# The output projection of a two-layer hybrid trunk, computed as seven quadrant products instead of one full product

## The chip, the cores and the metric

One core of one Trainium2 chip. The metric is the time of one execution on the device in microseconds (us); the median of several runs is compared. A profile is one such execution, recorded by the hardware profiler; its span goes from the first instruction to the last event.

## The reference

Two layers; each adds a mixer to the residual stream x of 512 tokens by 1024 features, all in float32:

```python
for l in range(2):
    h = rmsnorm(x, norm_g[l])
    p = h @ w_in[l]                       # 1024 -> 3488 columns, split into 15 parts
    o_a = causal attention (low-rank q and kv, rotary key)      # 256 columns
    o_b = c_b * short_conv(c_c * c_h)                           # 256
    o_c = spatial_gate(sg_u, sg_v)                              # 256
    o_d = block-sparse attention                                # 256
    y = concat(o_a * silu(g_a), o_b * silu(g_b), o_c * silu(g_c), o_d * silu(g_d))
    x = x + y @ w_out[l]                  # 512x1024 times 1024x1024
```

The change concerns the last line. Products have to keep nearly float32 precision.

## The kernel before, in words

**Numbers.** TensorE multiplies tiles of type fp32r, which hold fewer bits than float32. So each operand is split in two, `hi` (rounded by a copy into fp32r) and `lo` (the value less `hi`); `split2` (L245) does it with one copy on ScalarE (ACT) and one subtraction on VectorE (DVE). `mm3` (L250) then issues three matmuls for a product: hi by hi, hi by lo, lo by hi, all into one PSUM bank of 128 partitions by 512 columns.

**Layout.** Features lie on partitions: `hTh`, `hTl` hold the normed input h transposed, as 8 tiles of 128 features by 512 tokens. y is made the same way: `y_tiles` (L781) gives hi and lo of feature tile kt (0 and 1 from group A, 2 and 3 from B, 4 and 5 from C, 6 and 7 from D); `put_y` (L785) splits it and sets the event `L.y[kt]`. y4 to y7 come late; y5 is the last, made from `gc1`, the last product before the projection.

**Weights.** A `Unit` (L265) is a block of weights of up to 128x1024. `load_units` (L316) loads all units in one fixed order through two `raw` buffers (queue of SP), `split_units` (L331) splits each into one of six pairs `whi`, `wlo`, in halves of 512 columns: ACT makes `hi` (now and then DVE), DVE `lo`. A pair comes free when the last matmul that uses it is done. `w_out` is eight units per layer, `wo{half}{kq}`: half of the output columns, quarter of the features.

**The projection before** (L1229 to L1263): for each half of the output columns and each of four token tiles of 128, eight feature tiles times three matmuls of 512 columns, with y as the stationary and the weights as the moving operand: 192 matmuls per layer, into tiles named `o`. In the first half, token tiles 0 to 2 do six feature tiles first and the last two (y5, y7) afterwards. The very last token tile is cut into two passes of 256 columns. `out_chain` (L1145) then adds the bank to the residual tile `xr` on DVE; in layer 0 it also takes the sum of squares for the next norm (`square_half`, on ACT), stores x to DRAM and starts `pre_norm` (L544), which scales on DVE, transposes on TensorE and splits into `hTh`, `hTl`; in layer 1 it stores the output.

**Order.** A planner inside the kernel's Python code (`Order`, `Chain`, L58 to L193) writes out the order of the instructions on each engine. It has a clock per engine and a cost per instruction (TensorE n/2.4 + 2 ns, DVE 68 + 1.047 n, GpSimd 160 + 2.1 n, for n columns). Each chain of work is a generator that issues its next instruction when the clocks say that its input is nearly there. On the chip each engine works through its own list in that order and waits at semaphores. All instructions of DVE, ACT and GpSimd (POOL) are issued in one helper line, L158, those of TensorE (PE) in L184; so groups are told apart by their tiles.

**Buffers.** PSUM has three banks `acc`, two `tr` and three `s`, each handed out as slots. `t2` are nine 128x512 scratch tiles in SBUF; `tk` are two larger ones for Q and K of group A.

Of the kernel before, what the change touches and what calls it, by code (L numbers as in the profile page):

```python
# [38 lines left out]
YORDER, YCUT = (2, 3, 0, 1, 4, 6, 5, 7), 6  # L39
WORDER = (1, 0, 2, 3)  # L40
# [156 lines left out]
def hybrid_trunk(ctx: ExitStack, tc: tile.TileContext, x, positions, norm_g, w_c, w_f, w_t, w_o, mla_q_norm_g,  # L197
# [52 lines left out]
    def mm3(ch, n, dst, sh, sl, mh, ml, first, last):  # L250
        c = cost(n)
        yield from ch.pe(c, PE.matmul, dst, sh, mh, start=first, stop=False)
        yield from ch.pe(c, PE.matmul, dst, sh, ml, start=False, stop=False)
        yield from ch.pe(c, PE.matmul, dst, sl, mh, start=False, stop=last)
# [10 lines left out]
    class Unit:  # L265
        def __init__(self, src, a, b, name):
            self.src, self.a, self.b, self.name = src, a, b, name
            self.loaded, self.ready, self.wanted = Event(), Event(), False
            self.slots = eS if name[:-2] in EARLY else wS
# [31 lines left out]
    for l in range(DEPTH):  # L301
# [10 lines left out]
        for half in range(2):  # L312
            for kq in WORDER:
                add_unit(w_o[l, half, kq], 2, 512, f"wo{half}{kq}_{l}")

    def load_units():  # L316
        for u in order:
            ch = Chain(o)
            u.raw_slots = rawS
# [11 lines left out]
    def split_units():  # L331
        for u in order:
# [4 lines left out]
            for i in range(2):  # L337
# [11 lines left out]
                yield from c2.dve(V.tensor_tensor, lo, raw, hi.bitcast(F32), op=ALU.subtract)  # L349
            ch.t = c2.t  # L350
            u.raw_slots.put(ch)
            o.set(u.ready, ch.t)

# [27 lines left out]
    hTh = big.tile([P, KT, S], F32R, name="hTh")  # L381
    hTl = big.tile([P, KT, S], F32R, name="hTl")
# [128 lines left out]
    for l in range(DEPTH):  # L511
# [15 lines left out]
        L.mix_ev, L.mla_ev, L.QK_ev = Event(), Event(), Event()  # L527
        L.x = [None] * NT
# [15 lines left out]
    def pre_norm(L, t, xx, t0, release):  # L544
# [14 lines left out]
        if t == NT - 1:  # L559
            for _ in range(2):  # L560
                (t2S if L.l else sS).put(ch)

        def half(c):
            c2 = Chain(o, tps[c])
            tp = yield from trS.get(c2, f"hT{t}_{c}_{L.l}")
            for k in range(4):
# [3 lines left out]
            yield from split2(c2, hTh[:, c * 4:c * 4 + 4, t * P:(t + 1) * P],  # L570
                              hTl[:, c * 4:c * 4 + 4, t * P:(t + 1) * P], tp.rearrange("p (k n) -> p k n", k=4))
            trS.put(c2)
            o.set(L.hT[t][c], c2.t)
        for c in range(2):
            o.spawn(half(c))

# [79 lines left out]
    def q_chain(L, t, q_ps, t0):  # L656
        ch = Chain(o, t0)
        l = L.l
        if t == 0:
            L.Q = yield from tkS.get(ch, f"Q{l}", 96)  # L660
            L.K = yield from tkS.get(ch, f"K{l}", 96)
            o.set(L.QK_ev, ch.t)
# [122 lines left out]
    def put_y(ch, L, kt, yv):  # L785
        if kt == 6:
            L.yD = []
            for i in range(2):
                L.yD.append((yield from ydS.get(ch, f"yD{i}_{L.l}", [P, 2, S], F32R)))
        yield from split2(ch, *y_tiles(L, kt), yv)  # L790
        o.set(L.y[kt], ch.t)

# [352 lines left out]
    def out_chain(L, half, t, a, t0, c0=0, c1=512):  # L1145
        ch = Chain(o, t0)
# [4 lines left out]
        if l < DEPTH - 1:  # L1151
            yield from square_half(ch, layers[l + 1], t, half, a, L.x[t])
        accS.put(ch)
        if l == DEPTH - 1:
            nc.sync.dma_start(out[0, t * P:(t + 1) * P, cols], L.x[t][:, cols])
        elif half == 1:
            nc.sync.dma_start(x1d[t * P:(t + 1) * P, :], L.x[t])
            tend = ch.t + 4000.0

            def release(c):  # L1160
                c2 = Chain(o, max(c.t, tend))
                v4S.put(c2)
            o.spawn(pre_norm(layers[l + 1], t, L.x[t], ch.t, release))


    def main():
        m = Chain(o)

        def tok(L, n, width, t, dst, us):

            for k in range(KT):
                if n == "c" and k % 4 == 0:
                    yield from m.wait(L.hT[t][k // 4])
                if t == 0 and k % 2 == 0:
                    us.append((yield from unit(m, f"{n}{k // 2}_{L.l}")))
                wh, wlo = us[k // 2]
                yield from mm3(m, width, dst, hTh[:, k, t * P:(t + 1) * P], hTl[:, k, t * P:(t + 1) * P],
                               wh[:, k % 2, :], wlo[:, k % 2, :], k == 0, k == KT - 1)
                if t == NT - 1 and k % 2 == 1:
# [8 lines left out]
        for L in layers:  # L1188
# [8 lines left out]
            for t in range(NT):  # L1197
# [10 lines left out]
            for n in SEQ:  # L1208
# [10 lines left out]
                else:  # L1219
                    a = yield from accS.get(m, f"{n}_{l}")  # L1220
                    wh, wlo = yield from unit(m, f"{n}_{l}")
                    for k in range(KT):
                        yield from mm3(m, S, a, wh[:, k, :], wlo[:, k, :], hTh[:, k, :], hTl[:, k, :],
# [5 lines left out]
            for half in range(2):  # L1229
                us = {}  # L1230

                def part(t, a, i0, i1, c0=0, c1=512):
                    for i in range(i0, i1):
                        k = YORDER[i]
                        yield from m.wait(L.y[k])
                        if k // 2 not in us:
                            us[k // 2] = yield from unit(m, f"wo{half}{k // 2}_{l}")
                        wh, wlo = us[k // 2]
                        yh, yl = y_tiles(L, k)
                        yield from mm3(m, c1 - c0, a[:, c0:c1], yh[:, t * P:(t + 1) * P], yl[:, t * P:(t + 1) * P],  # L1240
                                       wh[:, k % 2, c0:c1], wlo[:, k % 2, c0:c1], i == 0, i == KT - 1)
                        if t == NT - 1 and c1 == 512 and all(x // 2 != k // 2 for x in YORDER[i + 1:]):
                            done_unit(f"wo{half}{k // 2}_{l}")
                        yield o.now

                acc = {}
                for group, cut in (((0, 1, 2), YCUT), ((3,), 0)) if half == 0 else (((t,), 0) for t in range(NT)):
                    for i0, i1 in ((0, cut), (cut, KT)):
                        for t in group:
                            if i0 == i1:  # L1250
                                continue
                            if i0 == 0:
# [130 lines left out]
```

## Time and profile before

| what | value |
|---|---|
| median of 3 runs | 508.73 us (508.62 to 508.78) |
| the profiled execution's own time | 508.65 us |
| span of its profile | 506.8 us |
| granted TensorE clock over the span | 0.996 |
| the first layer's projection in the trace | from 214.4 to 260.6 us |
| the second layer's projection in the trace | from 459.5 to 503.3 us |

A row of the page's groups reads: line, engine, operation, output and inputs by their names in the program, shapes, count, then busy time and the mean of one in ns, then the engine's idle time just before them and what ended it. PEld is TensorE's loading of the stationary operand, which runs beside the matmuls. In the rows of the timeline the first number is the start in the span, the second the time from the first to the last of the instructions merged into the row. Matmuls overlap, so their own durations are latencies and their pace is seen from their starts.

### The profile page before, as it was taken

Reading aid. Unit: us, or ns where it says so; the run is one execution under the profiler, and the core shown is the slowest. Engines: PE = TensorE matmul, PEld = TensorE weight load, DVE = VectorE, ACT = ScalarE, POOL = GpSimd, SP = SyncE. Lnnn points to the kernel's source line nnn. Section 1 sums busy time; section 2 is a strip of 40 time slices with the busy share of each in tenths; the row PEclk is TensorE's granted clock in tenths of the full one; section 3 lists DMA queues with packets and bytes.
Section 4 is the critical chain, followed back from the end, with each engine's and each line's share of the span. In section 5 each row is a group of like instructions: output and inputs, shape, how many; then the busy total and the mean of one; then the engine's idle time right before and its main releaser. Section 6 shows DMA issues by size and latency. Waiting matters only on the chain.

```text
span 506.8 us, 7665 instructions
## 1 busy us (share of the span) xinstructions
PE 498.1 (98%) x2508; PEld 423.3 (84%) x2508; DVE 349.3 (69%) x917; ACT 296.5 (58%) x891; POOL 139.2 (27%) x321
## 2 busy tenths in 40 slices
PE   6999999999999999999999999999999999999997
PEld 4898888888888888888889988888888888888886
DVE  4877975468799887635576988777868887635311
ACT  5698764567687775424247894677766777432100
POOL 6867875452000000000121488513330000000000
PEclk9999999999999999999999999999999999999999
DMA  8533415112114123464443242140142121624111
GB/s 273 165 123 114 125 43 166 41 43 66 60 43 166 52 74 109 142 175 117 143 155 126 83 125 71 55 124 2 42 167 82 43 83 49 201 84 164 66 54 50
DMA packets 20618, 51.57 MB, mean 102 GB/s; under 512 B 5985, under 2 KB 7265, under 8 KB 20578
## 3 DMA queue, kind: packets, MB, share of 16 engines
q1 hardware_dynamic: 20546, 51.08, 31.1%
q8 instruction: 20, 0.33, 0.3%
q0 software_dynamic: 32, 0.00, 0.1%
q14 instruction: 20, 0.16, 0.1%
HBM read 46.87 MB, written 4.19 MB: 101 GB/s over the span
## 4 chain that ended last, share of the span: by engine, by line
PE 90%; POOL 4%; DVE 2%; DMA 2%; ACT 1%; issue 1%; POOLq 0%; DVEq 0%
PE o L184 17%; PE kv L184 10%; PE cq L184 6%; PE sq L184 5%; PE cc L184 4%; PE gb L184 4%; PE cb L184 4%; PE gd L184 4%; PE gc L184 4%; PE ch L184 4%; PE su L184 4%; PE sa L184 3%; PE ga L184 3%; PE oa L184 2%; PE od L184 2%; PE sd L184 2%
## 5 line engine op out<-in xcount | busy, mean ns | idle before, releaser
L158 DVE TENSOR_TENSOR xr<-o,xr 128x512 f32<-128x512 f32 (+1 forms) x17 | 11.2, 658 | 42.0 <-PE o L184 42.0
L184 PE MATMUL o<-whi_wo,yTl 128*128 128x512 f32 (+1 forms) x102 | 38.4, 377 | 0.0
L184 PE MATMUL o<-wlo_wo,yTh 128*128 128x512 f32 (+1 forms) x102 | 38.4, 377 | 0.0
L184 PE MATMUL o<-whi_wo,yTh 128*128 128x512 f32 (+1 forms) x102 | 38.4, 376 | 0.0
L158 ACT ACTIVATE whi_wo<-raw_wo 128x512 fp32r<-128x512 f32 x31 | 18.3, 624 | 21.7 <-PE o L184 13.6
L158 ACT ACTIVATE pa<-pa,mna 128x256 f32<-128x256 f32 (+3 forms) x44 | 23.4, 539 | 5.2 <-DVE mna L158 5.1
L184 PE MATMUL kv<-whi_kv,hTh 128*128 128x512 f32 x64 | 26.0, 406 | 0.0
L184 PE MATMUL o<-whi_wo,yD 128*128 128x512 f32 (+1 forms) x68 | 25.7, 381 | 0.0
L158 ACT ACTIVATE pd<-pd,mnd 128x256 f32<-128x256 f32 (+3 forms) x46 | 24.5, 546 | 2.0 <-DVE mnd L158 1.5
L158 ACT ACTIVATE pha<-pTa 128x512 fp32r<-128x512 f32 (+3 forms) x32 | 13.9, 434 | 20.1 <-PE pTa L184 19.9
L184 PE MATMUL kv<-whi_kv,hTl 128*128 128x512 f32 x64 | 25.1, 392 | 0.0
L184 PE MATMUL kv<-wlo_kv,hTh 128*128 128x512 f32 x64 | 24.9, 390 | 0.0
L158 ACT ACTIVATE phd<-pTd 128x512 fp32r<-128x512 f32 (+3 forms) x32 | 13.9, 435 | 18.4 <-PE pTd L184 18.3
L184 PE MATMUL cq<-whi_c,hTh 128*128 128x416 f32 x64 | 24.3, 380 | 0.0
L184 PE MATMUL cq<-whi_c,hTl 128*128 128x416 f32 x64 | 23.3, 365 | 0.0
L184 PE MATMUL cq<-wlo_c,hTh 128*128 128x416 f32 x64 | 23.0, 360 | 0.0
L158 DVE TENSOR_TENSOR wlo_wo<-raw_wo,whi_wo 128x512 fp32r<-128x512 f32 x32 | 21.0, 687 | 2.4 <-ACT whi_wo L158 2.0
L184 PEld LDWEIGHTS o<-wlo_wo,yTh 128*128 128x128 f32 x102 | 19.2, 188 | 3.6
L184 PEld LDWEIGHTS o<-whi_wo,yTh 128*128 128x128 f32 x102 | 19.2, 188 | 3.6
L184 PEld LDWEIGHTS o<-whi_wo,yTl 128*128 128x128 f32 x102 | 19.2, 188 | 3.5
L158 DVE CUSTOM_DVE_ANT_0 pa<-sa,maskb 128x512 f32<-128x512 f32 (+3 forms) x32 | 15.0, 485 | 8.7 <-PE pTa L184 4.6
L158 DVE TENSOR_TENSOR pld<-pTd,phd 128x512 fp32r<-128x512 f32 (+3 forms) x32 | 15.5, 486 | 4.9 <-ACT phd L158 4.8
(328 smaller groups left out, 1712.8 us busy)
## 6 DMA issues: line engine op xcount, KB each, us to landing
raw_wo<-in_w_o_dram SPq DMA_DIRECT2D x16, 512.0 KB, 3.9
raw_sq<-in_w_t_dram SPq DMA_DIRECT2D x8, 512.0 KB, 3.5
raw_kv<-in_w_t_dram SPq DMA_DIRECT2D x8, 512.0 KB, 3.5
raw_c<-in_w_c_dram SPq DMA_DIRECT2D x8, 416.0 KB, 4.2
raw_ga<-in_w_f_dram SPq DMA_DIRECT2D x4, 512.0 KB, 3.6
raw_su<-in_w_f_dram SPq DMA_DIRECT2D x4, 512.0 KB, 3.5
raw_gc<-in_w_f_dram SPq DMA_DIRECT2D x4, 512.0 KB, 3.6
raw_ch<-in_w_f_dram SPq DMA_DIRECT2D x4, 512.0 KB, 3.4
```

Source lines behind the costliest of these rows:

```text
L158: f(*a, **k)
L184: f(*a, **k)
```

## The change

y is cut into four quadrants: A11 and A21 are feature tiles `K0` = (2, 3, 0, 1) for tokens 0 to 255 and 256 to 511, A12 and A22 feature tiles `K1` = (4, 6, 7, 5) for the same tokens. The weights are cut into B11, B12 (features of `K0`, first and second half of the columns) and B21, B22 (features of `K1`). The seven products of 256 tokens by 512 features by 512 columns are, by the names of their weight operands in `ZPROD`:

| product | stationary | moving |
|---|---|---|
| b11 | A11 | B11 |
| t3 | A11 − A21 | B22 − B12 |
| b21 | A12 | B21 |
| t2 | S2 = A22 − (A11 − A21) | T2 = B11 + t3's |
| t4 | A22 | B21 − T2 |
| t1 | S1 = S2 + A11 | B12 − B11 |
| b22 | A12 − S2 | B22 |

Each has two halves i of 128 tokens, and each half 4 feature tiles times three matmuls of 512 columns: 24 matmuls per product, 168 per layer. Each weight operand is two units, j = 0 and 1.

- **PSUM sums that run on.** b11, t3 and t4 write to the same two banks one after the other without clearing them, and so do t2, t1 and b22 with two others; after each product the sums as they stand are added to the rows of x to which they belong. b21 has banks of its own. So there are 16 adds of 128x512 per layer instead of 8. A product that continues in a bank waits until the adds of the product before it are done (`evs`).
- **Weight operands.** `z_load` loads the quarters (b11's into the `tk` tiles, some into space that h leaves free) and forms t3, t2, t4 and t1 by subtractions and additions of 128x512, in place. The `ew` helper puts each on GpSimd, unless DVE by the planner's clocks would be done more than 1200 ns earlier (for t4: if it would be done earlier at all). Each unit is then split as before; the `lo` of these units may go to GpSimd by the same rule with another constant. B12's and B22's quarters are loaded twice.
- **y operands.** `put_y` replaces tokens 256 to 511 of a tile of `K0` by the difference A11 − A21 before splitting. `s_chain` forms S2, S1 and A12 − S2 for each of the 4 pairs of tiles from the `hi` and `lo` parts: 3 + 2 + 2 instructions of 128x256 by `ew`, and three splits.
- **Space.** `hTh`, `hTl` become four tiles by halves of the features; after the last product of the layer that reads h, the sums of y lie in the first halves and weight quarters in the second ones. The next layer's h may be written there only when t1 is done (`h_done`).
- **Order of tokens.** Tokens 256 to 511 are finished after t1, tokens 0 to 255 after b22; the next layer's `cq` goes through the token tiles as 2, 3, 0, 1.
- **The end.** In layer 1 the last half product (b22, i = 1) goes in two passes of 256 columns to banks of its own; its running sum is added to x before that.

The core of the diff:

```diff
-YORDER, YCUT = (2, 3, 0, 1, 4, 6, 5, 7), 6
-WORDER = (1, 0, 2, 3)
+K0, K1 = (2, 3, 0, 1), (4, 6, 7, 5)
+ZPROD = ("b11", "t3", "b21", "t2", "t4", "t1", "b22")
+EWB, LOB = 1200.0, -600.0
...
-                yield from c2.dve(V.tensor_tensor, lo, raw, hi.bitcast(F32), op=ALU.subtract)
+                yield from ew(c2, lo, raw, hi.bitcast(F32), ALU.subtract, LOB if u.src is None else -1e9)
...
+    def ew(ch, out_, in0, in1, op, bias=EWB):
+        n = free_size(out_)
+        tv = max(o.clk["V"], ch.t, o.now) + 68 + 1.047 * n
+        tg = max(o.clk["G"], ch.t, o.now) + 160 + 2.1 * n
+        if tv + bias < tg:
+            yield from ch.dve(V.tensor_tensor, out_, in0, in1, op=op)
+        else:
+            yield from ch.pool(G.tensor_tensor, out_, in0, in1, op=op)
...
+    def z_load(u, kind, j, L):
...
+        elif kind == "t3":
...
+            w_quad(ch, l, 1, k0, halves(u.raw))
+            w_quad(ch, l, 1, k1, d)
+            def form():
+                c2 = Chain(o, ch.t)
+                for x, y in zip(d, halves(u.raw)):
+                    yield from ew(c2, y, x, y, ALU.subtract)
+                    t2S.put(c2)
+                o.set(u.loaded, c2.t)
+                yield from c2.wait(u.ready)
+                v = zu["t2"]
+                v.raw = u.raw
+                for x, y in zip(halves(zu["b11"].raw), halves(u.raw)):
+                    yield from ew(c2, y, x, y, ALU.add)
+                o.set(v.loaded, c2.t)
...
+        elif kind == "t4":
...
+                yield from c2.wait(zu["t2"].ready)
+                yield from c2.wait(zu["b21"].loaded)
+                u.raw, u.raw_slots = zu["t2"].raw, rawS
+                for x, y in zip(halves(zu["b21"].raw), halves(u.raw)):
+                    yield from ew(c2, y, x, y, ALU.subtract, 0.0)
...
+        if kt in K0:
+            yield from ew(ch, yv[:, 256:512], yv[:, 0:256], yv[:, 256:512], ALU.subtract)
         yield from split2(ch, *y_tiles(L, kt), yv)
         o.set(L.y[kt], ch.t)
+        if kt in K1:
+            o.spawn(s_chain(L, K1.index(kt)), None, 3)
...
+    def s_chain(L, kk):
...
+        yield from ew(ch, v, a22[0], s3[0], ALU.subtract)
+        yield from ew(ch, v, v, a22[1], ALU.add)
+        yield from ew(ch, v, v, s3[1], ALU.subtract)
+        c2 = Chain(o, ch.t)
+        yield from split2(c2, *s_place(L, "t2", kk), v)
+        o.set(L.s["t2"][kk], c2.t)
+        yield from ew(ch, z, v, a11[0], ALU.add)
+        yield from ew(ch, z, z, a11[1], ALU.add)
+        yield from split2(ch, *s_place(L, "t1", kk), z)
+        o.set(L.s["t1"][kk], ch.t)
+        yield from ch.wait(units[f"t41_{L.l}"].loaded)
+        yield from ew(ch, z, a12[0], v, ALU.subtract)
+        yield from ew(ch, z, z, a12[1], ALU.add)
+        yield from ch.wait(L.p2[kk])
+        yield from split2(ch, h1[:, 0:256], l1[:, 0:256], z)
...
+    def z_out(L, n, i, a, t0, ev, put):
+        ch = Chain(o, t0)
+        for t, half in {"b11": ((i, 0), (i, 1)), "t3": ((2 + i, 1),), "b21": ((i, 0),), "t4": ((2 + i, 0),),
+                        "t2": ((2 + i, 0),), "t1": ((2 + i, 1),), "b22": ((i, 1),)}[n]:
+            yield from add_out(ch, L, t, half, a, a if put else None)
+        o.set(ev, ch.t)
...
+            for n in ZPROD:
+                for i in range(2):
+                    ev = evs[n, i] = Event()
+                    if n == "b21":
+                        a = yield from sS.get(m, f"o{n}{i}_{l}")
+                        yield from prod(n, i, a, True)
+                        o.spawn(z_out(L, n, i, a, o.now + PELAT, ev, sS.put))
+                        continue
+                    c = n in ("b11", "t3", "t4")
+                    if n in ("b11", "t2"):
+                        X[c, i] = yield from (accS if c else sS).get(m, f"o{n}{i}_{l}")
+                    else:
+                        yield from m.wait(evs[{"t3": "b11", "t4": "t3", "t1": "t2", "b22": "t1"}[n], i])
...
+                    yield from prod(n, i, X[c, i], n in ("b11", "t2"))
+                    o.spawn(z_out(L, n, i, X[c, i], o.now + PELAT, ev,
+                                  {"t4": accS.put, "b22": sS.put}.get(n)))
```

More of the change, by code (lines that the diff above doesn't have):

```diff
@@ L558, in pre_norm @@
         release(ch)
[L559 removed]
+        if t == L.torder[-1]:
             for _ in range(2):
@@ L569, in half @@
             hput(c2)
[L570 to L571 removed]
+            if L.l:
+                yield from c2.wait(layers[L.l - 1].h_done[c])
+            if c not in L.h:
+                L.h[c] = [big.tile([P, 4, S], F32R, tag=f"h{x}{c}", name=f"hT{x}{c}_{L.l}") for x in "hl"]
+            yield from split2(c2, *(z[:, :, t * P:(t + 1) * P] for z in L.h[c]), tp.rearrange("p (k n) -> p k n", k=4))
             trS.put(c2)
```

231 lines of the change are left out of this document (167 added, 64 removed).

## The prediction

> **What bounds the kernel now.** I read the page from the top: first the engines' shares, then the chain that ended last, then the groups, then the chain in order of time around the two output projections.
>
> ```profile
> PE 498.1 (98%) x2508; PEld 423.3 (84%) x2508; DVE 349.3 (69%) x917; ACT 296.5 (58%) x891; POOL 139.2 (27%) x321
> ```
>
> ```profile
> PE 90%; POOL 4%; DVE 2%; DMA 2%; ACT 1%; issue 1%; POOLq 0%; DVEq 0%
> ```
>
> TensorE (PE) is busy 98% of the span and holds 90% of the chain. VectorE (DVE) has 31% to spare, GpSimd (POOL) 73%. So the kernel ends when TensorE has got through its matmuls, and only fewer or faster matmuls, or new gaps, move the end.
>
> ```profile
> 214.39 31.96 PE o L184 x141
> ...
> 247.22 5.47 PE o L184 x24
> ...
> 459.50 43.84 PE o L184 x216
> ```
>
> These pieces of the chain are the projections (tile `o`). The second layer's is one unbroken piece of 43.84 us; the first layer's is one with transposes for the next layer put in. A row of 24 matmuls takes 5.47 us, 0.228 us each. The second layer's piece is 168 matmuls 512 wide and 48 that are 256 wide (the last token tile is cut in two).
>
> ```profile
> 502.93 0.28 PE L184 MATMUL o<-wlo_wo,yD 128*128 128x256 f32 x1
> 503.05 0.28 PE L184 MATMUL o<-whi_wo,yD 128*128 128x256 f32 x1
> 503.37 0.42 DVE L158 TENSOR_TENSOR xr<-o,xr 128x256 f32<-128x256 f32 x1 [2.45 <-PE o L184]
> 503.82 0.33 SPq L1155 DMA_DIRECT2D out_dram<-xr  x1
> ```
>
> Narrow matmuls start every 0.12 us (the 0.28 is the latency, since they are pipelined), so 43.84 − 48 × 0.12 = 38.1 us are left for 168 wide ones: 0.227 each. After the last matmul come one add, one store and its landing, 3.4 us to the end at 506.8. The change leaves this tail as it is.
>
> ```profile
> core 0: us, PE busy (x) PEld busy (x) DVE busy (x) ACT busy (x) POOL busy (x), PEclk, DMA share, GB/s
> ...
> 214.39:260.61 46.22, 46.22 (x217) 38.47 (x217) 22.71 (x36) 15.80 (x34) 3.87 (x8) 1.00 0.47 144
> ...
> 459.50:506.80 47.30, 43.83 (x216) 37.08 (x215) 12.85 (x20) 5.74 (x10) 0.00 (x0) 1.00 0.24 87
> ```
>
> Busy times by stage, the two projections: TensorE has no gap, DVE is at 49% and 27%, POOL at 8% and 0, and the granted clock is full. That idle time is what the change spends.
>
> **What goes.** Seven products of 24 matmuls take the place of 192 per layer. The first layer loses 24 × 0.227 = 5.44 us. The second goes to 156 wide and 24 narrow: 35.4 + 2.9 = 38.3 against 43.84, 5.55 us. Together **−11.0 us**, if nothing makes TensorE wait. Transposes and everything before the projections keep their count.
>
> **What comes, per layer.** Price rows of one instruction:
>
> ```profile
> L158 DVE TENSOR_TENSOR xr<-o,xr 128x512 f32<-128x512 f32 (+1 forms) x17 | 11.2, 658 | 42.0 <-PE o L184 42.0
> ...
> L158 ACT ACTIVATE whi_wo<-raw_wo 128x512 fp32r<-128x512 f32 x31 | 18.3, 624 | 21.7 <-PE o L184 13.6
> ...
> L158 DVE TENSOR_TENSOR wlo_wo<-raw_wo,whi_wo 128x512 fp32r<-128x512 f32 x32 | 21.0, 687 | 2.4 <-ACT whi_wo L158 2.0
> ```
>
> ```profile
> 211.67 1.89 DVE L158 TENSOR_TENSOR wlo_wo<-raw_wo,whi_wo 128x512 fp32r<-128x512 f32 x3
> ...
> 301.79 0.43 DVE L158 TENSOR_TENSOR vnl<-vn,vnh 128x256 fp32r<-128x256 f32 x1 [0.44 <-ACT vnh L158]
> ```
>
> In a row of three a 512-wide DVE instruction costs 0.63 us (1.89/3); for a 256-wide one I take 0.38, the 0.43 less the same overlap. Counted from the diff: weight units 14 instead of 8, so 12 more splits on ACT (7.5 us) and DVE (7.6); 16 adds out of PSUM instead of 8 (+5.0 DVE); 16 weight sums 512 wide; 4 differences and 28 sums of y, 256 wide; 12 splits of y sums, 256 wide (4.6 DVE). ACT goes from 15.8 to some 28 of 38 us: covered. The rows for loads:
>
> ```profile
> GB/s 273 165 123 114 125 43 166 41 43 66 60 43 166 52 74 109 142 175 117 143 155 126 83 125 71 55 124 2 42 167 82 43 83 49 201 84 164 66 54 50
> ...
> raw_wo<-in_w_o_dram SPq DMA_DIRECT2D x16, 512.0 KB, 3.9
> ```
>
> The weight quarters grow from 4 to 6 MB per layer, so 2 MB more in 38 us, some 53 GB/s on top of 144 or 87, where the page's first slice moved 273: covered as well. On SP's queue a quarter that waits for its buffer holds up what stands behind it (stores of `x1d` and `out`, the next layer's `c` units); these have a product or more to spare, so I charge nothing; without that cover it would be up to a load, 3.9 us to landing, once.
>
> No sum this large stands on POOL in the trace. Nearest are its two-input rows at 32 and 64 columns:
>
> ```profile
> 315.03 0.25 POOL L158 TENSOR_TENSOR mq<-mq,cosT 128x32 f32<-128x32 f32 x1
> ```
>
> ```profile
> 292.69 0.32 POOL L158 TENSOR_TENSOR rbq<-Q,sinT 128x64 f32<-128x64 f32 x1
> ```
>
> The slope is 0.07 us in 32 columns, 2.2 ns a column, on 0.18 fixed: estimates 0.74 us at 256 and 1.3 us at 512, with ends at half (overlapped) and double (blocked).
>
> Before a projection starts, the sums for t3, the differences of y and in the second layer those for t2 find DVE and POOL half empty: nothing charged. All else falls between the start T and T + 34.7, when b22's first half reaches its last operand (6 × 5.44 + 3 × 0.68). In that time DVE has 20 weight splits (12.6), 12 y splits (4.6), the end of y5 (two more, 1.3), t4's 4 sums (2.5: their bias is 0, so DVE) and 14 adds (8.8), 29.8 in all; to that come as I guess a quarter of the 28 y sums (2.7), because the planner turns to DVE when POOL is about a microsecond behind. POOL has the other 21 (15.5) and t1's four (5.2), 20.7. Taken singly both fit: DVE 32.5, POOL 20.7, of 34.7.
>
> **What speaks against it** is that the two engines get in each other's way:
>
> ```profile
> 305.18 0.28 DVE L158 SCALAR_TENSOR_TENSOR mq<-mq,mmq,dq_b 128x64 f32<-128x64 f32 x1
> ...
> 306.67 0.92 DVE L158 SCALAR_TENSOR_TENSOR mq<-mq,mmq,dq_b 128x64 f32<-128x64 f32 x2
> ```
>
> ```profile
> 306.62 0.61 POOL L158 COPY K<-krt 128x512 f32<-128x512 f32 x1
> ```
>
> ```profile
> 263.74 0.63 POOL L158 TENSOR_SCALAR_AFFINE_SELECT sgw<-sgw 128x512 f32<-128x512 f32 x1
> 263.81 1.12 DVE L158 SCALAR_TENSOR_TENSOR h<-xr,xss,ng 128x512 f32<-128x512 f32 x1 [0.45 <-POOL xss L158]
> ...
> 265.32 0.74 DVE L158 SCALAR_TENSOR_TENSOR h<-xr,xss,ng 128x512 f32<-128x512 f32 x1
> ```
>
> Two DVE instructions that take about 0.25 each beside small work took 0.92 beside POOL's copy; one of 0.74 took 1.12 beside POOL's select, and ended 0.56 after it, as if started when POOL let go. All have both inputs in SBUF, as every split of a weight or sum has; adds out of PSUM have one. The Trainium skill, "SBUF — State Buffer", section "Who interferes with whom", makes the port pair of VectorE and GpSimd an exclusive lock; by that rule all the two-input work would stand in one line. These rows agree with it.
>
> If the two exclude each other for whole durations, DVE's two-input work (21.0 + 2.7) and POOL's 20.7 make one line of 44.4 us against 34.7: 9.7 late. If only the part that grows with the columns excludes (DVE 0.26 us in 256 columns, from 0.69 less 0.43; POOL 2.2 ns a column), it is 20 × 0.52 + 12 × 0.26 + 2 × 0.52 + 4 × 0.52 + 7 × 0.26 = 18.5 and 21 × 0.56 + 4 × 1.13 = 16.3: 34.8, just in time. For the latter speaks a short pair:
>
> ```profile
> 316.69 0.26 POOL L158 TENSOR_TENSOR mq<-mq,cosT 128x32 f32<-128x32 f32 x1
> ```
>
> ```profile
> 316.76 0.48 DVE L158 SCALAR_TENSOR_TENSOR mq<-mq,mmq,dq_b 128x64 f32<-128x64 f32 x2 [1.19 <-POOL mmq L158]
> ```
>
> Two DVE instructions beside a short POOL one kept their 0.24 each. I take the second reading and add what uneven demand costs: the y sums crowd into the first ten microseconds, b21's splits are queued among them and are due at T + 10.9, t2's at T + 16.3. The first new wait is earlier: t3's first half continues in b11's bank and waits for two adds (1.3 us) in the 2.72 us that b11's second half takes, while DVE ends y5:
>
> ```profile
> 460.17 0.69 DVE L158 SCALAR_TENSOR_TENSOR th_gc<-th_gc,gc 128x512 f32<-128x512 f32 x1 [1.49 <-ACT th_gc L158]
> ...
> 462.55 0.69 DVE L158 TENSOR_TENSOR yTl<-u,yTh 128x512 fp32r<-128x512 f32 x1
> ```
>
> That is T + 0.7 to T + 3.7; the adds are ready at T + 2.8 and due at T + 5.4. Queued behind them are b21's splits. I take 0.5 us for this wait and 2.5 for late operands of b21, t2 and b22: **3 us per layer, +6.0**; ends 0 and 9.7 per layer.
>
> **Between the layers.** Token tiles 2 and 3 are now done first, after t1, and the next layer's `cq` begins with tile 2. The way from the last matmul to split `hT`, before:
>
> ```profile
> 241.62 0.69 DVE L158 TENSOR_TENSOR xr<-o,xr 128x512 f32<-128x512 f32 x1 [2.37 <-PE o L184]
> ...
> 244.23 1.41 DVE L158 SCALAR_TENSOR_TENSOR h<-xr,xss,ng 128x512 f32<-128x512 f32 x2 [0.92 <-POOL xss L158]
> ...
> 248.66 0.68 DVE L158 TENSOR_TENSOR hTl<-hT,hTh 128x512 fp32r<-128x512 f32 x1
> ```
>
> 241.6 to 249.3 is 7.7 us, of which the first half of the features needs 6.5. Before, tile 0 had three token tiles (16 us) to cover it; now tile 2 has three half products, 8.2. That nearly covers it; for DVE's queue I take **+0.8**, ends 0 and 3.
>
> **Sum**: −11.0 + 6.0 + 0.8 = −4.2. The profiled execution took 508.65 (span 506.8 and 1.85 around it), 0.08 below the median of 508.73, so the sum carries over: **504.5 us**.
>
> **Rivals.** (1) *No hindrance*: POOL's sums fill its idle time and the splits run beside them. For it: each engine's load fits; against it: the rows at 263 and 306. 508.65 − 11.0 + 0.8 gives 498.5 to 501.5. Chance 0.22. (2) *POOL's sums lock out the splits*, the other side: as soon as the line of two-input work makes each projection over 5.1 us late, it is slower. At the full 9.7 it gives 508.65 − 11.0 + 19.4 + 0.8 = 517.9, at 6 per layer 510.5. For it: DVE ended 0.56 after the select; against it: the short pair, and the sums that can be early. Chance 0.28. (3) *The hand-over between the layers* fails as well: 3 us instead of 0.8 and 4 per layer, 508.7; with 3 per layer 506.7. Chance 0.08. (4) *The change does not do what it says*: fewer matmuls, but TensorE's starts spread because the waits at each shared bank fall between matmuls, and the 11 us return as gaps: 508.7. Chance 0.04. The forecast, 501.5 to 507.7, has 0.38.
>
> A measurement here tells 0.2%, 1 us, from no change. Faster: 0.38 + 0.22 + half of (3) = 0.64. Same: 0.04 + 0.04 = 0.08. Slower: 0.28. The range runs from 499 to 513, cutting off the bottom of (1) and the upper part of (2); the forecast's own is 501.5 to 507.7.
>
> **What would show it.** 168 matmuls per projection still 0.227 us apart; TensorE idle in the two projections of some 6 us, put down to DVE (adds before t3, `wlo_` of b21 and t2, y sums); DVE splits of 512 columns with a mean clearly above 0.69 beside POOL sums of about 1.3 us. If the splits stay at 0.69, rival 1 is right; if a split beside a POOL sum takes 1.5 us or more and gaps of over 5 us stand ahead of t2 or b22, rival 2. The forecast also falls if the planner gave DVE most of the y sums, or if a DMA is what TensorE waits for.

## The result and the profile after

The changed kernel takes 523.51 us (median of 4 runs, 523.09 to 524.37) against 508.75 for the kernel before (508.62 to 509.13): the ratio is 1.0291, 95% interval 1.0273 to 1.0309. It is slower by 15 us where 4 us less were forecast, and the stated range ended at 513. The profiled execution took 523.09, with a span of 521.4.

First the shares of the engines and the chain by engine, from the page of the changed kernel:

```profile
PE 497.2 (95%) x2448; PEld 416.8 (80%) x2448; DVE 420.6 (81%) x990; ACT 318.5 (61%) x940; POOL 232.6 (45%) x408
...
PE 78%; DVE 11%; DMA 3%; ACT 3%; issue 2%; POOL 2%; SPq 0%; DVEq 0%; ACTq 0%; POOLq 0%
```

TensorE runs 60 matmuls fewer than the 2508 of before, yet its busy time is nearly what it was. Its share of the chain fell from 90% to 78%, and DVE's rose from 2% to 11%. DVE is busy 71 us more, POOL 93 us more.

The busy times over the two projections (from the start to the preparations of the next `cq`, and from the start to the last matmul) show where that is:

```profile
core 0: us, PE busy (x) PEld busy (x) DVE busy (x) ACT busy (x) POOL busy (x), PEclk, DMA share, GB/s
214.35:264.60 50.25, 42.17 (x159) 32.03 (x158) 49.19 (x65) 22.55 (x50) 38.93 (x36) 0.90 0.37 114
470.20:517.65 47.45, 41.25 (x181) 33.08 (x179) 43.07 (x58) 16.75 (x34) 31.34 (x29) 0.93 0.31 106
```

In the first layer DVE is busy for 49.19 of 50.25 us and POOL for 38.93. TensorE, which had no gap before, is idle for 8.1 and 6.2 us. From the first matmul of the first layer's projection to the first of the next `cq` it was 46.1 us and is 53.6 (+7.5); from there to the second projection +3.2; the second projection took 43.7 and takes 47.6 us (+3.8). With 0.1 ahead of the first projection that makes the 14.6 by which the span grew. Against the pace without waits (168 matmuls at 0.227 us; in the second 156 of these and 24 narrow ones at 0.12) the first projection is 14.7 us late and the second 9.4, counted by the starts of its matmuls, the transposes between them taken off.

How a gap looks, in TensorE's timeline (start, duration; the idle time before and its releaser in brackets):

```profile
219.56 0.39 PE L185 MATMUL ob<-whi_b,yTl 128*128 128x512 f32 x1
222.03 0.47 PE L185 MATMUL ob<-whi_t,yTh 128*128 128x512 f32 x1 [2.08 <-DVE xr L159]
...
223.59 0.63 PE L185 MATMUL ob<-whi_t,yTh 128*128 128x512 f32 x1
224.02 0.63 PE L185 MATMUL ob<-wlo_t,yTh 128*128 128x512 f32 x1
```

t3 waits for b11's adds to x, and DVE is late with them. And there is a second loss: from 223.59 on matmuls start every 0.43 us instead of every 0.227. The windows show the same as a lower granted clock (PEclk, 1.00 is full):

```profile
219.96:223.37 3.41, 1.34 (x6) 1.15 (x7) 3.41 (x6) 2.18 (x6) 3.41 (x4) 1.00 0.96 336
223.38:226.78 3.40, 2.97 (x8) 1.77 (x6) 3.40 (x5) 1.83 (x4) 3.40 (x3) 0.50 0.49 113
247.27:250.68 3.41, 1.33 (x4) 0.58 (x4) 3.30 (x6) 2.55 (x6) 3.41 (x4) 1.00 0.26 67
250.69:254.09 3.40, 3.40 (x8) 2.58 (x9) 3.40 (x6) 0.24 (x1) 0.42 (x1) 0.50 0.75 259
```

TensorE is "busy" for the whole of the last stretch, but passes 8 matmuls where 0.227 us each would give 15. In the two projections 27 matmuls follow the one before at the slow pace, about 5.4 us (27 × 0.2), of which 3.8 lie in the first layer. A busy share alone hides this; the count and PEclk beside it show it.

Why DVE is late stands in its own timeline and groups:

```profile
218.87 1.22 DVE L159 TENSOR_TENSOR wlo_t<-raw_t,whi_t 128x512 fp32r<-128x512 f32 x1
220.01 0.68 DVE L159 TENSOR_TENSOR xr<-ob,xr 128x512 f32<-128x512 f32 x1
220.61 0.68 DVE L159 TENSOR_TENSOR yTl<-u,yTh 128x512 fp32r<-128x512 f32 x1
221.21 0.68 DVE L159 TENSOR_TENSOR xr<-ob,xr 128x512 f32<-128x512 f32 x1
```

```profile
L159 DVE TENSOR_TENSOR wlo_t<-raw_t,whi_t 128x512 fp32r<-128x512 f32 x24 | 26.0, 1108 | 0.1
L159 DVE TENSOR_TENSOR suml<-s,sumh 128x256 fp32r<-128x256 f32 x16 | 16.0, 1021 | 0.0
L159 DVE TENSOR_TENSOR wlo_b<-spareh,whi_b 128x512 fp32r<-128x512 f32 x16 | 14.3, 918 | 0.0
L159 DVE TENSOR_TENSOR xr<-ob,xr 128x512 f32<-128x512 f32 x20 | 13.6, 680 | 1.3 <-PE ob L185 1.2
```

The split of a weight took 0.69 us before; now the first row's 24 take 1.11 and the third row's 16 take 0.92. The split of a sum, 256 wide, takes 1.02 where 0.42 is its time alone (the `yTl` of the same size in this trace). The add `xr`, with one input in PSUM, keeps its 0.68. One such piece on both engines:

```profile
235.76 1.51 DVE L159 TENSOR_TENSOR suml<-s,sumh 128x256 fp32r<-128x256 f32 x1
237.19 0.74 DVE L159 TENSOR_TENSOR raw_t<-spareh,raw_t 128x512 f32<-128x512 f32 x1
237.86 1.52 DVE L159 TENSOR_TENSOR suml<-s,sumh 128x256 fp32r<-128x256 f32 x1
```

```profile
235.20 1.78 POOL L159 TENSOR_TENSOR raw_b<-sparel,raw_b 128x512 f32<-128x512 f32 x1
237.07 0.51 POOL L159 TENSOR_SCALAR gq_b<-gq_b 128x96 f32<-128x96 f32 x1
237.66 1.43 POOL L159 TENSOR_TENSOR raw_b<-sparel,raw_b 128x512 f32<-128x512 f32 x1
```

Each split of 256 columns ends 0.3 us after the POOL sum beside it; the sum of 512 columns between them, which for most of its time met only a small POOL instruction, took 0.74.

### The profile page after: what moved, and what is told of

It reads as the page before. It is cut to its first block, busy times and chain, and to the rows that moved or that the text cites. A ratio compares the mean times of both kernels' runs of the same rounds, so it can differ in the third digit from the quotient of the medians.

```text
span 521.4 us, 7838 instructions
## 1 busy us (share of the span) xinstructions
PE 497.2 (95%) x2448; PEld 416.8 (80%) x2448; DVE 420.6 (81%) x990; ACT 318.5 (61%) x940; POOL 232.6 (45%) x408
## 3 DMA queue, kind: packets, MB, share of 16 engines
q1 hardware_dynamic: 25154, 55.27, 32.5%
## 4 chain that ended last, share of the span: by engine, by line
PE 78%; DVE 11%; DMA 3%; ACT 3%; issue 2%; POOL 2%; SPq 0%; DVEq 0%; ACTq 0%; POOLq 0%
PE kv L185 9%; PE sq L185 8%; PE cq L185 5%; PE cb L185 4%; PE cc L185 4%; PE gb L185 4%; PE gd L185 4%; PE ch L185 4%; PE su L185 4%; PE ga L185 4%; PE gc L185 4%; PE ob L185 3%; DVE suml L159 3%; PE sa L185 3%; PE ot L185 3%
## 5 line engine op out<-in xcount | busy, mean ns | idle before, releaser
L159 POOL TENSOR_TENSOR chs<-chs 128x256 f32<-128x256 f32 x4 | 3.3, 815 | 52.4 <-DVE chs L159 52.4
L159 DVE TENSOR_TENSOR wlo_t<-raw_t,whi_t 128x512 fp32r<-128x512 f32 x24 | 26.0, 1108 | 0.1
L159 ACT ACTIVATE whi_t<-raw_t 128x512 fp32r<-128x512 f32 x24 | 14.5, 622 | 18.3 <-DVE raw_t L159 12.2
L185 PE MATMUL kv<-whi_kv,hTl 128*128 128x512 f32 x64 | 25.1, 392 | 0.0
L159 POOL TENSOR_TENSOR s<-s,yTl 128x256 f32<-128x256 f32 x23 | 24.5, 1083 | 0.1
L159 ACT ACTIVATE pa<-pa,mna 128x128 f32<-128x128 f32 (+3 forms) x43 | 22.5, 533 | 2.4 <-DVE mna L159 2.3
L159 POOL TENSOR_TENSOR raw_t<-d0t,raw_t 128x512 f32<-128x512 f32 x4 | 5.9, 1470 | 33.4 <-DMA d0t<-in_w_o_dram 14.0
L159 DVE TENSOR_TENSOR pla<-pTa,pha 128x512 fp32r<-128x512 f32 (+3 forms) x32 | 15.2, 483 | 5.3 <-ACT pha L159 5.2
L185 PE MATMUL sq<-yTh,hTh 128*128 128x512 f32 x48 | 18.9, 393 | 0.0
L185 PE MATMUL sq<-yTh,hTl 128*128 128x512 f32 x48 | 18.7, 391 | 0.0
L185 PE MATMUL sq<-yTl,hTh 128*128 128x512 f32 x48 | 18.7, 390 | 0.0
```

Source lines behind the costliest of these rows:

```text
L159: f(*a, **k)
L185: f(*a, **k)
```

## The experiments

**Theory** (exclusion): a DVE instruction with two inputs in SBUF and a POOL instruction exclude each other, and DVE's list, kept in order, is stretched by what POOL does. **Rivals**: the queue theory, in which TensorE waits because of the number and order of instructions in DVE's list and not because of an exclusion; and the shared banks, where t3's wait for b11's adds, in whose bank it continues, is what costs. The changed kernel is called C. Times are medians; the kernel before took 509.02 to 509.19 us beside these runs.

| run | us | ratio to before (95%) | first projection to next cq | second projection |
|---|---|---|---|---|
| before | 508.75 | 1 | 46.1 | 43.7 |
| C | 523.51 | 1.0291 (1.0273–1.0309) | 53.6 | 47.6 |
| e2 no sums | 504.38 | 0.9906 (0.9883–0.9928) | 42.2 | 40.5 |
| e7 no sums, bank copies | 498.45 | 0.98 (0.9775–0.9826) | 39.4 | 38.1 |
| e3 sums on DVE | 521.86 | 1.0261 (1.0237–1.0286) | 49.0 | 48.9 |
| e6 bank copies | 525.23 | 1.0317 (1.0292–1.0343) | 53.3 | 48.1 |
| e5 PSUM splits | 516.53 | 1.015 (1.0127–1.0173) | 53.7 | 41.8 |
| e8 both | 513.5 | 1.0088 (1.0069–1.0106) | 46.6 | 43.5 |
| e9 both, sums on POOL | 516.19 | 1.014 (1.0122–1.0158) | 49.5 | 44.4 |
| e10 both, early sums | 511.53 | 1.0047 (1.003–1.0063) | 46.1 | 43.2 |
| e11 early sums alone | 518.27 | 1.0181 (1.0165–1.0197) | 50.3 | 45.5 |
| e12 e10, t3 by PSUM too | 505.48 | 0.9927 (0.9909–0.9944) | 43.6 | 39.5 |

(The last two columns run between starts of matmuls: the first of the projection, and the first of the next `cq` or the last of the projection.)

**e1: the two engines side by side.** The kernel before, with a stretch added behind its end that measures the pair alone; its 717.68 us include the stretch.

```diff
+        dv(20, n, q[2], q[3])
+        po(10, n)
+        meet()
+        dv(20, n, pb, q[3])
+        po(10, n)
...
+    for n in (0, 1, 2, 3, 4, 6, 8, 12):
+        for i in range(48):
+            PE.matmul(pc, st, mv, start=i == 0, stop=i == 47)
...
+        for i in range(n):
+            V.tensor_tensor(q[4], q[4], q[2], op=ALU.add)
```

`dv` issues additions of n columns on DVE (`q` lies in SBUF, `pb` in PSUM), `po` on POOL, `meet` lets each engine wait for the other; behind them come bursts of 48 matmuls with pauses of growing length.

> The kernel before, with a stretch added behind its end that works on scratch tiles: (a) additions of 512 and of 256 columns with both inputs in SBUF, alone on VectorE, then alone on GpSimd, then side by side without any dependency between the two, then side by side with one of VectorE's inputs in PSUM; (b) bursts of 48 matmuls with a growing pause between them. Exclusion theory (the two engines shut each other out while both need SBUF for two inputs): side by side, an addition of 512 columns that takes 0.6 to 0.69 us alone on VectorE takes 1.1 us or more and one of 1.3 us on GpSimd 1.7 or more; with one input in PSUM both return to their times alone. Queue theory (the long VectorE rows of the changed kernel contain waiting for operands that GpSimd and ScalarE deliver late): side by side both keep the times they have alone, in all stretches. For the bursts: after a pause of over 2 us the matmuls start about 0.43 us apart for some 3 us, as after the gaps of the changed kernel; after a short pause 0.227.

DVE's timeline (6 alone; 20 two-input beside 10 of POOL; 20 with an input in PSUM beside 10 of POOL), and POOL's:

```profile
507.08 4.26 DVE L1350 TENSOR_TENSOR q<-q,q 128x512 f32<-128x512 f32 x6
...
520.88 23.94 DVE L1350 TENSOR_TENSOR q<-q,q 128x512 f32<-128x512 f32 x20
...
545.67 14.47 DVE L1350 TENSOR_TENSOR q<-pb,q 128x512 f32<-128x512 f32 x20
```

```profile
512.03 8.12 POOL L1354 TENSOR_TENSOR g<-g,g 128x512 f32<-128x512 f32 x6
...
520.72 16.28 POOL L1354 TENSOR_TENSOR g<-g,g 128x512 f32<-128x512 f32 x10
...
545.45 13.35 POOL L1354 TENSOR_TENSOR g<-g,g 128x512 f32<-128x512 f32 x10
```

And the windows of the side-by-side stretch:

```profile
core 0: us, PE busy (x) PEld busy (x) DVE busy (x) ACT busy (x) POOL busy (x), PEclk, DMA share, GB/s
520.88:537.20 16.32, 0.77 (x4) 0.30 (x2) 16.01 (x10) 0.00 (x0) 15.42 (x10) 0.67 0.00 0
```

Alone a DVE instruction takes 0.71 us and a POOL one 1.35. Side by side ten pairs take 16.28, 1.63 a pair on the mean, one for one: while POOL's ten ran, DVE got through ten of its twenty, and the other ten took 0.71 each. With one input in PSUM neither noticed the other (0.72 and 1.335). So the exclusion is real, and a pair costs 1.63, more than POOL's 1.35 and less than the 2.06 of both durations. The same stretch at 256 columns (0.45 and 0.787 alone) gives the parts that grow with the columns: 0.52 and 1.13, as the prediction had them. Their sum, 1.65, is about what a pair costs; so it is these parts that add. The Trainium skill, "SBUF — State Buffer", section "Who interferes with whom", says that a DVE instruction with at most one SBUF input does not contend, which these rows confirm, and calls the shared port pair an exclusive lock. Held for whole durations the lock would make a pair 2.06; the measured 1.63 decides against reading it so.

The bursts missed the expectation. TensorE's timeline:

```profile
622.84 11.17 PE L1374 MATMUL pc<-mv,st 128*128 128x512 f32 x48 [2.50 <-DVE st L1378]
637.23 11.18 PE L1374 MATMUL pc<-mv,st 128*128 128x512 f32 x48 [3.22 <-DVE st L1378]
652.36 12.77 PE L1374 MATMUL pc<-mv,st 128*128 128x512 f32 x48 [3.95 <-DVE st L1378]
670.53 14.05 PE L1374 MATMUL pc<-mv,st 128*128 128x512 f32 x48 [5.41 <-DVE st L1378]
```

After 2.5 or 3.2 us of idle time nothing is lost; after 3.95 a burst is 1.6 us longer, after 5.41 2.9.

**e2: no sums.** The sums of weights and y aren't formed; the splits read unsummed quarters.

```diff
     def ew(ch, out_, in0, in1, op, bias=EWB):
+        if bias >= 0.0:
+            return
...
-            yield from split2(c2, *s_place(L, "t2", kk), v)
+            yield from split2(c2, *s_place(L, "t2", kk), a22[0])
...
```

> The changed kernel without its 48 sums per layer (weights and y): each split reads a quarter as it is, so the products and the number of splits stay and the results mean nothing. Both theories: the sums are what is too much, so TensorE has next to no gaps in the projections: 508.7 - 11.0 + 1 to 3 us for the hand-over between the layers = 498.5 to 501; VectorE's splits of weights back at 0.69 us. If the splits alone, or the 16 adds per layer and the waits at the shared banks, were the fault, it stays above 508.

504.38 is 19 us below C, but 3 to 6 above what was expected. What is left in the projections are four gaps of 0.5 to 1.3 us, all ahead of t3; counted from start to start they are 4.65 us longer than the pace. One of them in TensorE's timeline:

```profile
221.21 0.50 PE L185 MATMUL ob<-whi_t,yTh 128*128 128x512 f32 x1 [1.16 <-DVE xr L159]
```

So the wait at the shared bank costs something even without sums. e6 and e7 test it.

**e3: all sums on DVE.**

```diff
-        if tv + bias < tg:
+        if True:
```

> All sums of the changed kernel on VectorE, none on GpSimd. Exclusion: VectorE's own work in the critical stretch is 20 splits, 12 small splits, 14 adds, 28 small sums and 8 to 10 large ones, 44 us of 34.7, but nothing is stretched any more: 8 to 10 us late per layer, about what the two engines reach now: 514 to 524 us, splits at 0.69. Queue: VectorE, busy all through already, gets some 20 us more of work per layer (23 sums of 256 and 6 of 512 columns at least): over 535 us.

521.86, as the exclusion had it. The groups of DVE and a window at the start of the first projection:

```profile
L159 DVE TENSOR_TENSOR wlo_t<-raw_t,whi_t 128x512 fp32r<-128x512 f32 x24 | 16.2, 683 | 0.0
...
L159 DVE TENSOR_TENSOR suml<-s,sumh 128x256 fp32r<-128x256 f32 x16 | 6.5, 417 | 0.0
```

```profile
214.35:250.00 35.65, 29.72 (x124) 23.52 (x123) 35.65 (x76) 16.12 (x35) 3.34 (x2) 0.95 0.51 145
```

With POOL empty the splits are back at 0.683 and 0.417, though DVE runs without a break. DVE got through 76 instructions in this window (C: 41 in 35.5 us, and POOL's 33 beside them). So the sums cost DVE no more if it forms them itself than if POOL forms them beside it: POOL's help is worth nothing here.

**e6: bank copies.** ACT copies b11's banks to free ones; the adds read the copies, and t3 waits for ACT alone.

```diff
+        if n == "b11":
+            cp = yield from sS.get(ch, f"cp{i}_{L.l}")
+            yield from ch.act(A.activation, cp, a, AF.Copy)
+            o.set(ev, ch.t)
+            a = cp
```

> The changed kernel, but ScalarE copies b11's two banks into two free ones at once, and the four adds of b11 read the copies; so t3 waits for ScalarE's copy and no longer for VectorE's adds. In the changed kernel TensorE stands some 7 us in all before t3 (2.1 and 2.8 us in the first layer, 2.0 in the second), and runs at half pace behind it. Theory that VectorE's two-input work is the bound: the gap only moves on to b21 and t2, whose operands come no earlier; 520 to 524 us. Theory that the shared bank is a cause by itself: these gaps vanish for good, 514 to 518 us.

525.23: no gain, the gaps move on to the next late operands (the longest are now 2.6 us in b21 and, in the second layer, 4.3 in t2, both for a split). DVE remains busy throughout (35.62 of the 35.65 us from 214.35 to 250).

**e7: bank copies and no sums** (e2 and e6 together).

> The kernel without sums (results mean nothing) with the same copies of b11's banks. Without sums TensorE had two gaps of some 1.2 us per layer, all before t3, 4.65 us in all. If they were the shared bank's and nothing else: 499.5 to 500.5 us, and no gap over 0.5 us in the projections. If VectorE's row of instructions only hands them on: 503 to 505.

```profile
214.35:250.00 35.65, 35.65 (x159) 29.52 (x158) 30.46 (x53) 22.88 (x52) 4.74 (x7) 1.00 0.55 161
```

498.45 with no gap and full clock: 159 matmuls in this window, transposes included, where C had 104. The projections' count is worth what was forecast. Between e2 and e7 lie 5.9 us, 5.2 of them in the two stretches of the table (42.2 to 39.4, 40.5 to 38.1): the price of the shared bank when DVE isn't the bound. e6 shows that it can't be had while DVE is.

**e5: splits by way of PSUM.** ACT also copies the weights of b21, t2, t4, t1 and b22 into a PSUM bank, and DVE subtracts `hi` from that copy, with one input in SBUF. POOL keeps its sums.

```diff
+                if u.name[:-3] in PSPLIT:
+                    pc = (yield from trS.get(c2, f"pc{i}{u.name}"))[:, :n // 2]
+                    yield from c2.act(A.activation, pc, raw, AF.Copy)
+                    yield from c2.act(A.activation, hi, raw, AF.Copy)
+                    yield from c2.dve(V.tensor_tensor, lo, pc, hi.bitcast(F32), op=ALU.subtract)
+                    trS.put(c2)
+                    continue
```

> The changed kernel, but for the units b21, t2, t4, t1 and b22 ScalarE copies the weights into a PSUM bank as well, and VectorE forms lo from that copy and hi, so that the instruction has one input in SBUF. ScalarE gets 20 x 0.6 = 12 us more per layer, VectorE as many instructions as before. Exclusion: these 20 splits run beside GpSimd's sums, at 0.69 instead of 1.1 us, and GpSimd is blocked only by y's small splits: 6 to 8 us less late per layer, 505 to 513 us. Queue: nothing gets shorter, ScalarE's extra work makes it later: 523 to 530 us.

The groups of DVE:

```profile
L160 DVE TENSOR_TENSOR wlo_t<-pc1t,whi_t 128x512 fp32r<-128x512 f32 x12 | 8.2, 683 | 1.7 <-ACT whi_t L160 1.5
...
L160 DVE TENSOR_TENSOR wlo_t<-raw_t,whi_t 128x512 fp32r<-128x512 f32 x8 | 7.4, 956 | 0.0
```

Splits that read PSUM take 0.683 beside POOL's sums, those left in SBUF 0.956. This is the exclusion shown inside the kernel, at the same count of DVE instructions. At 516.53 the size falls short of the expected one: the second projection is down from 47.6 to 41.8, but the first layer's still takes 53.7. Waits of 2.1 us ahead of t3 and 2.0 in t2 remain there, and the next layer's transposes use the same two banks as the copies; as TensorE's timeline shows:

```profile
260.72 0.66 PE L186 MATMUL hT<-ident,h 128*128 128x128 f32 x4 [2.25 <-DVE hTl L160]
261.99 1.11 PE L186 MATMUL hT<-ident,h 128*128 128x128 f32 x4 [0.61 <-DVE wlo_b L160]
```

The transposes wait 2.25 us for the split of earlier ones (`hTl`) to free a bank, then 0.61 for a weight's split (`wlo_b`) that holds the other.

**e8: both** (e6's copies and e5's splits; in the first layer only for b21, t2 and t4, so that the banks are free for the transposes).

> Both remedies in the real computation: copies of b11's banks by ScalarE, and lo formed from a PSUM copy (b21, t2, t4 in both layers, t1 and b22 in the second only, since in the first the next layer's transposes need the same two banks). In the second layer the projection was 3.6 us over its 38.2 with the second remedy alone, of them some 2 before t3: now 39 to 41 us. In the first, without the fight for banks, some 44 to 48 instead of 53.7. Exclusion theory: 503 to 510 us. If it is the amount of work of VectorE that binds: 514 to 520.

513.5, above the expected span. The largest wait left, in TensorE's timeline, is for b21:

```profile
231.88 0.50 PE L186 MATMUL ob<-wlo_b,yD 128*128 128x512 f32 x1 [3.10 <-DVE wlo_b L160]
```

Its split stands in DVE's list behind adds and behind sums and splits of y, which still have both inputs in SBUF (a `suml` takes 0.659 us on the mean instead of 0.42).

**e9: e8 with every sum on POOL** (`if tv + bias < tg:` becomes `if bias < 0.0:`).

> As e8_both, with every sum of weights and y on GpSimd. VectorE is rid of its two-input sums (each up to 1.5 us long beside GpSimd), but GpSimd's line grows to some 28 x 0.79 + 10 x 1.35 = 36 us per layer, more than the 34.7 there are. Exclusion theory: GpSimd becomes the bound, 2 to 6 us later than e8_both. If VectorE's volume binds: 2 to 6 us earlier.

516.19, 2.7 later than e8: more sums for POOL make it slower, though DVE is then busy for 27.35 us of the window from 214.35 to 250 instead of 34.63. A count of DVE's load would have had it faster.

**e10: e8 with early sums.** S2 and S1 of the first three pairs of tiles are formed before the space for their splits is free, that is before the projection.

```diff
-        yield from ch.wait(L.hT_free)
...
+        if L.hT_free.t is None:
+            yield from ew(ch, z, v, a11[0], ALU.add)
+            yield from ew(ch, z, z, a11[1], ALU.add)
+            yield from ch.wait(L.hT_free)
```

> As e8_both, but S2 and S1 of the three pairs whose y is known early are formed before the projection begins, when VectorE and GpSimd have room, and only their splits wait for the space. That takes 15 of the 28 y sums per layer, some 9 to 11 us of work of both engines, out of the critical stretch. Exclusion theory: what is left there is 13 y sums, t1's four on GpSimd and t4's on VectorE; GpSimd some 15 us, VectorE's waits for it halved: 503 to 509 us, the second layer's projection at 39 to 41 us. If the splits and adds of VectorE alone bind: 511 to 514.

511.53, a gain of 2 us only. The collision moved, as DVE's timeline ahead of the projection shows:

```profile
212.67 3.52 DVE L160 TENSOR_TENSOR wlo_t<-raw_t,whi_t 128x512 fp32r<-128x512 f32 x3
```

Three of t3's splits take 3.52 us, 1.17 each, beside the sums that now stand there.

**e11: C with the early sums alone.**

> The changed kernel with the early y sums and neither of the other two remedies. Exclusion theory: 9 to 11 us of two-input work less per layer in the critical stretch, but some of it would have run beside the adds: 508 to 516 us. If it is the shared bank and the splits: 521 to 524.

518.27: 5.2 us better than C, but 2 above the span that was expected. The waits gather ahead of t3, where TensorE stands 7.9 us for DVE's `xr` in the first layer. Moving the sums brings 5.2 us, taking the splits out of their way 7.0 (e5), and neither alone makes up C's 15.

**e12: e10 with t3's splits by way of PSUM too** ("t3" added to both lists).

> As e10_early, and t3's splits also take lo from a PSUM copy, since in the first layer they meet GpSimd's sums for t2 just before the projection (three splits took 2.98 us in the changed kernel). Exclusion theory: another 1 to 2 us: 502 to 508. Otherwise as e10_early, or later by ScalarE's 8 more copies.

The page and the windows:

```profile
PE 490.1 (97%) x2448; PEld 412.7 (82%) x2448; DVE 400.0 (79%) x986; ACT 339.9 (67%) x981; POOL 227.4 (45%) x415
```

```profile
214.35:250.00 35.65, 33.41 (x140) 25.37 (x139) 34.34 (x53) 28.08 (x60) 25.07 (x26) 1.00 0.50 145
460.00:500.00 40.00, 39.57 (x183) 32.22 (x182) 34.52 (x58) 29.33 (x58) 21.20 (x21) 1.00 0.37 125
```

505.48: with the same sums formed and POOL issuing no fewer instructions than in C (415 for 408) the scheme is faster than C and, by 0.7%, than the kernel before. In the same first window 140 matmuls start instead of C's 104, at full clock; the projections take 43.6 and 39.5 us. Of the 25.1 us between C and the kernel without sums or bank wait (e7), 18 are recovered.

## Why the prediction was wrong

**What goes, −11.0**: right. e7, which forms no sums and copies b11's banks away, shows it: 0.98 of the time before, 10.6 us less, with the hand-over in it.

**Loads**: nearly right. POOL's sums were estimated at 0.74 and 1.3 us and take 0.787 and 1.35 alone (e1). DVE's own load was put at 32.5 us per layer. In C it is busy for 49.2 and 43.1; taking from each group what it took over its time alone (mean less 0.685 for 512 columns, less 0.42 for 256, times the count) gives 16.1 and 12.7 us of stretch, and 33.1 and 30.4 are left. A term is missing from POOL's column, though: in the first layer t2's four weight sums don't all stand ahead of the projection. POOL forms them from 212.62 on, the last two at 220.64 and 225.54, after the start at 214.35:

```profile
220.64 1.77 POOL L159 TENSOR_TENSOR raw_t<-raw_b,raw_t 128x512 f32<-128x512 f32 x1
```

The second layer's were done by 470.13, when the projection began. This may be part of why the first layer lost 14.7 us and the second 9.4; no run tries it. No load of weights ends a wait of TensorE in the projections. ACT ends two, both in the first layer, of 0.62 and 1.14 us, the second after ACT itself had stood 5.06 us for DVE's `xr`:

```profile
249.43 0.50 PE L185 MATMUL ob<-whi_t,yD 128*128 128x512 f32 x1 [1.14 <-ACT whi_t L159]
```

**The price of the exclusion**: right by the pair (0.52 + 1.13, measured 1.63), and the second of the two readings was the right one.

**"34.8, just in time"**: this is the step that failed. The line that I summed held only the two-input parts of DVE's work, 18.5, and POOL's, 16.3. It left out DVE's other 14.0 us: the fixed parts and the adds, which don't exclude but stand in the same list, in order, and can run beside POOL only when no split stands ahead of them. DVE's own 32.5 and POOL's 16.3 are 48.8, if none of it is hidden, 14.1 more than the 34.7 there were; DVE was in fact busy for 49.2 in the first layer and 43.1 in the second, 16.1 and 12.7 of it stretch, so DVE's list paid for next to all of POOL's 16.3 in the first layer and for most of it in the second. e3 bears that out: with POOL's sums in DVE's own list the time is about the same. To a line of 34.8 with 34.7 to spend I added 3 us; measured are 14.7 and 9.4 of lost time per layer.

**The clock** wasn't in the sum. Of the 24.1 us lost, 5.4 are matmuls at half pace behind gaps; what the total would be with the gaps and full clock was not tried.

**The shared bank, 0.5 per layer**: too small, since the adds wait in DVE's list like all else. Its price without sums is the 5.2 us between e2 and e7 in the stretches of both layers.

**The hand-over, +0.8**: the size came out near, by another cause, which is luck. In e7 TensorE has no gap over 0.2 us between the first projection's start and the end of the next `cq`: DVE's queue costs nothing there. In C the next `cq` grew by 3.2 us, of which some 1.8 are 16 transposes that moved into it (a row of 8 took 0.87 us) and 1.0 is a gap that stands in TensorE's timeline and, with its cause, in POOL's:

```profile
276.46 0.66 PE L185 MATMUL hT<-ident,h 128*128 128x128 f32 x4 [1.00 <-DVE hTl L159]
```

```profile
273.24 1.26 POOL L159 TENSOR_SCALAR_AFFINE_SELECT sgw<-sgw 128x512 f32<-128x512 f32 x1 [1.35 <-DMA sgw<-in_sg_w_dram]
```

POOL stood 1.35 us for the load of `sgw`, and the small instruction that `h` needs stood behind it; the prediction had charged loads at nothing.

**The rivals**: rival 2 came true: POOL's sums held up the splits, and each projection was more than 5.1 us late. Of its two signs the first was there: beside POOL sums three splits of weights took 1.77 us in the projections. The second was not: no gap was over 5 us. The longest three are 2.76 us within t3, 2.37 within t2 and 2.08 ahead of t3; the loss is spread over ten gaps and the slow matmuls behind them. Its 517.9 counted 9.7 per layer and no clock; with 14.7 and 9.4 the sum is 508.65 − 11.0 + 24.1 + 1.0 = 522.8, against the profiled 523.09.

**Why matmuls fell to half pace** in C after 2.1 us of idle time, when in e1 3.2 us did no harm, the traces themselves answer. In each of them the granted clock changes only at points of a grid 3.41 us apart, and it follows how busy TensorE was in the stretch before such a point, not how long one gap was. C's 2.08 us lie within one stretch, 219.96 to 223.37 in the windows above, which leaves TensorE busy for 1.34 of 3.41 us, and the next stretch has half the clock. From 247.27 on gaps of 0.50, 1.14 and 0.66 us do the same together (1.33 us busy). e1's 3.22 us are shared by two stretches, each busy for more than half, and the clock stays full:

```profile
632.27:635.68 3.41, 1.74 (x8) 1.12 (x6) 1.56 (x3) 0.00 (x0) 0.00 (x0) 1.00 0.00 0
635.69:639.09 3.40, 1.86 (x8) 1.56 (x9) 1.42 (x3) 0.00 (x0) 0.00 (x0) 1.00 0.00 0
```

Over the kept traces of all 13 runs, a stretch at full clock in which TensorE was busy for less than 0.48 of the time was followed by one at half clock in 26 cases of 26; above 0.60 the clock stayed full in all of 1856; between the two it went both ways. The Trainium skill, "TensorE: Matmul & The Clock Gate", Part 1, gives an idle window of about 3.4 us that runs freely. The grid agrees with that; that a stretch need not be idle throughout is what these traces add. Open stays what lies behind the cases between 0.48 and 0.60.

## What to carry to other kernels

When work is moved from VectorE to GpSimd, count not the load of each engine but VectorE's list plus the streaming part of every GpSimd instruction with SBUF inputs that falls beside a two-input one; if that is more than the stage has, the engine that was meant to be relieved becomes the bound. Before giving up such a scheme, look for an engine that can put one of VectorE's inputs into PSUM: here ACT's copies, together with earlier sums and copies of the shared bank, turned 1.029 into 0.993. Ask of each gap on TensorE also what the matmuls behind it cost.

## What the hardware showed beside that

The pair alternates strictly one for one, so the exclusion costs the longer list nothing more once the shorter one has ended: the last ten of e1's twenty DVE additions took 0.71 us each. At 256 columns it is the same in small: ten pairs take 8.48 us, where POOL alone takes 0.787 an instruction and DVE 0.45. POOL suffers as well: its 512-wide sums `raw_b` took 1.62 in C for 1.35 alone.
